# Low parts of the down-projection weights: by a VectorE subtraction, or by a negation and an adding transfer

## The chip, the cores and the metric

The kernel runs on one core of one Trainium2 chip. The metric is the device time of one execution in microseconds, the median of three runs. A profiled execution, taken once more by the hardware profiler, gives the trace that is read here.

## The reference, cut to what matters

The program is a two-layer encoder trunk over 256 frames of width 2048, all in float32. Each layer is a norm, an attention mixer and a residual, then a norm, a gated convolution FFN and a residual. The change lies in the second matrix of the FFN, `w_down`, of 5632 x 2048, in both layers:

```python
def _conv_ffn(xn, w_up, conv_w, conv_b, w_down):
    up = xn @ w_up
    u, g = up[..., :D_FF], up[..., D_FF:]
    g = lax.conv_general_dilated(g, conv_w[:, None, :], window_strides=(1,),
    ...
    return (jax.nn.silu(g) * u) @ w_down
```

## The kernel before

Every large matrix product is made of three products of rounded operands. A float32 operand is split into a high part, its value rounded to the type float32r, and a low part, the float32 value less the high part. TensorE then adds up high x high, high x low and low x high into one PSUM bank. The activations are split once per stage. The weights are streamed from HBM and split as they come, in `stream` (lines 122 to 149).

`stream` loads four k tiles of a weight block at a time, 128 partitions x 4 x 512 float32 (1 MB), into a `raw` buffer (line 130, issued on SP; three buffers rotate). It then goes over the block in steps of two k tiles (KC = 2). In the form that the down product uses, ScalarE copies the two k tiles into `hi` (line 140), a tile of type float32r, and VectorE subtracts `hi` from `raw` into `lo` (line 141). The pool `wsplit` has four buffers for `hi` and four for `lo`, and all weight streams of the kernel share them in order. So the split of a step can begin when the products of the step four before it have read their buffers.

`gemm_tok` (lines 151 to 173) does the products of a step: for each of its two k tiles and each of the two token tiles three matmuls of 512 columns, on lines 158 (high activations, `hi`), 159 (high activations, `lo`) and 160 (low activations, `hi`). These are 12 matmuls per step. The up product runs in `gemm_feat` (lines 183 and 185), with the same `stream`.

In `ffn` (lines 253 to 307) the 5632 hidden features are cut into six groups, five of 1024 and one of 512. `up_group` makes the hidden values of a group: ScalarE copies the side half out of PSUM (line 272), VectorE adds it (line 274), POOL multiplies by the norm factor into `un` (line 276), ScalarE, VectorE and ScalarE do the convolution and the gate (lines 280 to 286), and the result is split into `hT` (lines 287 and 288). `down_group` multiplies a group's `hT` by its rows of `w_down`, for four column blocks of 512, and VectorE adds each block's sum to the residual `h` (line 298). The order in the program is up group 0, then for each next group its up product followed by the down product of the group before, and at the end the last group's down product. A down group of 1024 features has 2 blocks of 1 MB per column block, which are 8 loads and 16 steps; the last one, of 512 features, has 4 loads and 8 steps and follows the fifth one without an up product between. In both layers together these are 88 loads and 176 steps. The last column block of the last group of layer 1 takes its token tiles one after the other (`tok_first`).

The order of instructions on each engine is set when the program is built, by a scheduler that follows the program's order and a simulated timeline. Each engine then works through its own queue in order; SP's queue holds the loads, and POOL's queue holds `un`, the small `pow` operations of the norms and two loads at the start (`pos_i` and `vecs`, lines 368 and 413).

Of the kernel before, what the change touches and what calls it, by code (L numbers as in the profile page):

```python
# [11 lines left out]
F32 = mybir.dt.float32  # L12
F32R = mybir.dt.float32r
I32 = mybir.dt.int32
AF = mybir.ActivationFunctionType
ALU = mybir.AluOpType
# [10 lines left out]
KC = 2  # L27
KD = 4
# [20 lines left out]
def kernel(  # L49
# [7 lines left out]
    vec, act, pool, pe = nc.vector, nc.scalar, nc.gpsimd, nc.tensor  # L57
# [19 lines left out]
    def bank_tile(use, shape, name):  # L77
        pools = turn[use]
        turn[use + "_n"] += 1
        return pools[turn[use + "_n"] % len(pools)].tile(shape, F32, tag=use, name=name)  # L80
# [38 lines left out]

    last = {}  # L120

    def stream(name, src, nk, gain=None, pieces=1, before=None):

        for k0 in range(0, nk, KD):
            raw = wraw.tile([P, KD, CB], F32, tag="raw", name=f"raw_{name}_{k0}")
            for i in range(0, KD, KD // pieces):
                if before:
                    before(k0 + i, KD // pieces)
                part = slice(i, i + KD // pieces)
                last["dma"] = nc.sync.dma_start(raw[:, part, :], src[k0 // KD, :, part, :])  # L130
            for i in range(0, KD, KC):
                nm = f"{name}_{k0 + i}"
                hi = wsplit.tile([P, KC, CB], F32R, tag="whi", name=f"whi_{nm}")
                lo = wsplit.tile([P, KC, CB], F32R, tag="wlo", name=f"wlo_{nm}")
                if gain is None and pieces == KD:
                    for j in range(KC):
                        act.copy(hi[:, j, :], raw[:, i + j, :])
                        vec.tensor_tensor(lo[:, j, :], raw[:, i + j, :], hi[:, j, :].bitcast(F32), ALU.subtract)
                elif gain is None:
                    act.copy(hi, raw[:, i:i + KC, :])  # L140
                    vec.tensor_tensor(lo, raw[:, i:i + KC, :], hi.bitcast(F32), ALU.subtract)  # L141
                else:
                    for j in range(KC):
                        k = k0 + i + j
                        g = gain[:, k:k + 1]
                        act.activation(hi[:, j, :], raw[:, i + j, :], AF.Copy, scale=g)  # L146
                        vec.scalar_tensor_tensor(lo[:, j, :], raw[:, i + j, :], g, hi[:, j, :].bitcast(F32),  # L147
                                                 ALU.mult, ALU.subtract)
                yield k0 + i, hi, lo

    def gemm_tok(name, xt, nk, src, gain=None, pieces=1, before=None, tok_first=False):

        acc = bank_tile("acc", [P, NT, CB], f"acc_{name}")

        def products(k, t, hi, lo):
            xh = xt[:, k, t * P:(t + 1) * P]
            xl = xt[:, k, S + t * P:S + (t + 1) * P]
            pe.matmul(acc[:, t, :], xh, hi, start=k == 0, stop=False)  # L158
            pe.matmul(acc[:, t, :], xh, lo, start=False, stop=False)  # L159
            pe.matmul(acc[:, t, :], xl, hi, start=False, stop=k == nk - 1)  # L160

        steps = ((k0 + j, hi[:, j, :], lo[:, j, :])
                 for k0, hi, lo in stream(name, src, nk, gain, pieces, before) for j in range(KC))
        if tok_first:
            steps = list(steps)
            for t in range(NT):
                for k, hi, lo in steps:
                    products(k, t, hi, lo)
        else:
            for k, hi, lo in steps:  # L170
                for t in range(NT):
                    products(k, t, hi, lo)
        return acc

    def gemm_feat(name, xt, src, pairs, gain=None):

        accs = [bank_tile("acc", [P, 2, CB], f"acc_{name}_{i}") for i in range(len(pairs))]
        for k0, hi, lo in stream(name, src, KT, gain):
            for acc, pair in zip(accs, pairs):
                for m, c in enumerate(pair):  # L180
                    for j in range(KC):
                        k = k0 + j
                        pe.matmul(acc[:, m, :], hi[:, j, c * P:(c + 1) * P], xt[:, k, :],  # L183
                                  start=k == 0, stop=k == KT - 1, skip_group_check=True)
                        pe.matmul(acc[:, m, :S], lo[:, j, c * P:(c + 1) * P], xt[:, k, :S],  # L185
                                  start=False, stop=k == KT - 1, skip_group_check=True)
        return accs
# [55 lines left out]
    def shifted(pool, tag, name, k, shift):  # L243

        t = pool.tile([P, k * 2 * S + PAD], F32R, tag=tag, name=name)
        o = shift // 4
        return t[:, o:o + k * 2 * S].rearrange("p (k s) -> p k s", k=k)
# [5 lines left out]
    def ffn(l, xt, rb, then):  # L253
        up, dn = ((ffn_w_up0, ffn_w_down0), (ffn_w_up1, ffn_w_down1))[l]
        cc = ccols[l]
        groups, f = [], 0
        for n in (4, 4, 4, 4, 4, 2):
            groups.append((f, n))
            f += n
        assert f * 256 == DFF  # L260
        with tc.tile_pool(name=f"ffn{l}", bufs=2) as fp:
            def up_group(gi):
                b0, n = groups[gi]
                hT = shifted(fp, "hT", f"hT{l}_{gi}", 8, HT_SHIFT)
                for b in range(b0, b0 + n):
                    accs = gemm_feat(f"up{l}_{b}", xt, up[b], [(0, 2), (1, 3)])
                    for i, acc in enumerate(accs):
                        ft = 2 * b + i
                        r = 2 * (b - b0) + i
                        nm = f"{l}_{ft}"  # L270
                        side = fp.tile([P, 2, S], F32, tag="side", name=f"side{nm}")
                        act.copy(side, acc[:, :, S:])
                        ug = fp.tile([P, 2, S], F32, tag="ug", name=f"ug{nm}")
                        vec.tensor_tensor(ug, acc[:, :, :S], side, ALU.add)  # L274
                        un = fp.tile([P, 2, S], F32, tag="un", name=f"un{nm}")
                        pool.tensor_tensor(un, ug, rb.unsqueeze(1).broadcast_to([P, 2, S]), ALU.mult)  # L276
                        gn = un[:, 1, :]
                        cv = fp.tile([P, S], F32, tag="cv", name=f"cv{nm}")
                        w = lambda j: cc[:, j * NF + ft:j * NF + ft + 1]
                        act.activation(cv, gn, AF.Identity, scale=w(2), bias=w(3))  # L280
                        vec.scalar_tensor_tensor(cv[:, 1:], gn[:, :S - 1], w(1), cv[:, 1:], ALU.mult, ALU.add)
                        vec.scalar_tensor_tensor(cv[:, 2:], gn[:, :S - 2], w(0), cv[:, 2:], ALU.mult, ALU.add)  # L282
                        sg = fp.tile([P, S], F32, tag="sg", name=f"sg{nm}")
                        act.activation(sg, cv, AF.Silu)  # L284
                        hh = fp.tile([P, S], F32, tag="hh", name=f"hh{nm}")
                        vec.tensor_tensor(hh, sg, un[:, 0, :], ALU.mult)
                        act.copy(hT[:, r, :S], hh)
                        vec.tensor_tensor(hT[:, r, S:], hh, hT[:, r, :S].bitcast(F32), ALU.subtract)
                return hT

            def down_group(gi, hT):
                b0, n = groups[gi]
                for c in range(NB):
                    end = l == 1 and gi == len(groups) - 1 and c == NB - 1
                    acc = gemm_tok(f"dn{l}_{gi}_{c}", hT, 2 * n, dn[c, b0 // 2:(b0 + n) // 2], tok_first=end)
                    for t in range(NT) if end else (slice(0, NT),):
                        hs = h[:, t, c * CB:(c + 1) * CB]
                        vec.tensor_tensor(hs, acc[:, t, :], hs, ALU.add)  # L298
                        if gi == len(groups) - 1:
                            then(c, t)  # L300

            prev = up_group(0)
            for gi in range(1, len(groups)):
                cur = up_group(gi)
                down_group(gi - 1, prev)
                prev = cur
            down_group(len(groups) - 1, prev)
# [57 lines left out]
    with tc.tile_pool(name="mixa", bufs=2) as ap, tc.tile_pool(name="mixa1", bufs=1) as ap1:  # L365
# [12 lines left out]
        for rnd in range(2):  # L378
# [4 lines left out]
            n = ap1.tile([P, NT, 16], F32, name=f"turns_n{rnd}")  # L383
# [171 lines left out]
    with banks("f0", "acc"):  # L555
        _, rb = norm_factor("xf0")
# [85 lines left out]
    with banks("f1", "acc"):  # L642
        _, rb = norm_factor("xf1")
# [67 lines left out]
```

## Time and profile before

| what | value |
|---|---|
| median of 3 runs | 2268.43 us (2267.75 to 2269.35) |
| the profiled execution, its own time | 2269.63 us |
| its span, first to last instruction | 2267.8 us |
| busy: TensorE / VectorE / ScalarE / POOL | 2255.9 / 1443.7 / 1163.3 / 216.9 us |
| mean granted clock of TensorE | 0.999 |
| moved by DMA | 419.85 MB, mean 185 GB/s |

The span is read from the trace, and the execution's own time is 1.8 us longer than it. Busy time counts the instructions of an engine; weight loads of TensorE (PEld) overlap its matmuls (PE). Matmuls overlap each other too: one lasts 0.39 us in the trace, while the next one starts 0.23 us after it. The granted clock is the share of full speed that TensorE was given. "DMA share" is how busy the core's 16 DMA engines were on average.

### The profile page before, as it was taken

To read this page: it belongs to the slowest core of one execution; us is meant where nothing else is said; L and a number is where in the kernel's file an instruction comes from. 1 tells how busy PE (TensorE), PEld (TensorE's weight loads), DVE (VectorE), ACT (ScalarE), POOL (GpSimd) and SP (SyncE) were. 2 spreads that over 40 slices of the span, in tenths; PEclk is the share of its full clock that TensorE was granted. 3 is DMA by queue.
4 is the path that set the end of the run, shared out by engine and by line. 5 is a ranking of instruction groups with operands and counts; after the bars stand their busy time and mean duration, and the time that the engine had idled before them with its cause. 6 is when DMAs were issued, how large, how long until landed. Compare 5 with 4: busy or idle time off the path is not lost.

```text
span 2267.8 us, 29308 instructions
## 1 busy us (share of the span) xinstructions
PE 2255.9 (99%) x11616; PEld 1919.5 (85%) x11616; DVE 1443.7 (64%) x1873; ACT 1163.3 (51%) x1603; POOL 216.9 (10%) x214
## 2 busy tenths in 40 slices
PE   8999999999999999999999999999999999999999
PEld 7888888888888888888888888888888888888887
DVE  8676765666666566666665555556676665757664
ACT  6544455555445454544456756645554444535442
POOL 3111100011000000100001111001110000101000
PEclk9999999999999999999999999999999999999999
DMA  8455445555555555555544454455555555555654
GB/s 285 171 180 173 167 158 183 182 188 191 195 186 186 186 197 193 186 188 189 198 169 166 169 183 169 167 186 173 199 181 193 190 194 190 186 188 183 204 186 149
DMA packets 63210, 419.85 MB, mean 185 GB/s; under 512 B 7072, under 2 KB 9248, under 8 KB 13408
## 3 DMA queue, kind: packets, MB, share of 16 engines
q1 hardware_dynamic: 62816, 417.40, 53.7%
q8 instruction: 91, 1.49, 0.3%
q0 software_dynamic: 112, 0.39, 0.1%
q14 instruction: 47, 0.39, 0.0%
q10 hardware_dynamic: 144, 0.18, 0.0%
HBM read 415.85 MB, written 2.10 MB: 184 GB/s over the span
## 4 chain that ended last, share of the span: by engine, by line
PE 98%; DVE 1%; DMA 1%; ACT 0%; issue 0%; SPq 0%; DVEq 0%
PE acc_up L183 29%; PE acc_up L185 15%; PE acc_dn L158 7%; PE acc_dn L160 7%; PE acc_dn L159 7%; PE acc_k L183 3%; PE acc_q L183 2%; PE acc_k L185 1%; PE acc_bv L158 1%; PE acc_k L159 1%; PE acc_k L158 1%; PE acc_k L160 1%; PE acc_v L158 1%; PE acc_bv L159 1%; PE acc_v L160 1%; PE acc_bv L160 1%
## 5 line engine op out<-in xcount | busy, mean ns | idle before, releaser
L183 PE MATMUL acc_up<-xf,whi_up 128*128 128x512 f32 x2816 | 984.7, 396 | 0.6 <-DVE xf L214 0.6
L185 PE MATMUL acc_up<-xf,wlo_up 128*128 128x256 f32 x2816 | 782.5, 280 | 0.0
L141 DVE TENSOR_TENSOR wlo_up<-raw_up,whi_up 128x1024 fp32r<-128x1024 f32 x352 | 439.2, 1248 | 320.6 <-ACT whi_up L140 320.5
L183 PEld LDWEIGHTS acc_up<-xf,whi_up 128*128 128x128 f32 x2816 | 526.7, 188 | 124.0 <-PE pt_rs_xf L235 0.8
L140 ACT CAST whi_up<-raw_up 128x1024 fp32r<-128x1024 f32 x352 | 369.0, 1048 | 353.2 <-PE acc_up L183 282.6
L185 PEld LDWEIGHTS acc_up<-xf,wlo_up 128*128 128x128 f32 x2816 | 531.4, 189 | 3.5
L141 DVE TENSOR_TENSOR wlo_dn<-raw_dn,whi_dn 128x1024 fp32r<-128x1024 f32 x176 | 217.9, 1238 | 161.7 <-ACT whi_dn L140 161.7
L140 ACT CAST whi_dn<-raw_dn 128x1024 fp32r<-128x1024 f32 x176 | 185.2, 1052 | 242.2 <-PE acc_dn L160 183.1
L160 PE MATMUL acc_dn<-whi_dn,hT 128*128 128x512 f32 x704 | 274.3, 390 | 0.0
L158 PE MATMUL acc_dn<-whi_dn,hT 128*128 128x512 f32 x704 | 274.3, 390 | 0.0
L159 PE MATMUL acc_dn<-wlo_dn,hT 128*128 128x512 f32 x704 | 274.3, 390 | 0.0
L276 POOL TENSOR_TENSOR un<-ug,rsb_xf 128x512 f32<-128x512 f32 x88 | 121.4, 1380 | 1218.6 <-DVE ug L274 1218.6
L160 PEld LDWEIGHTS acc_dn<-whi_dn,hT 128*128 128x128 f32 x704 | 132.2, 188 | 27.5
L158 PEld LDWEIGHTS acc_dn<-whi_dn,hT 128*128 128x128 f32 x704 | 132.2, 188 | 27.4
L159 PEld LDWEIGHTS acc_dn<-wlo_dn,hT 128*128 128x128 f32 x704 | 132.2, 188 | 27.1
L284 ACT ACTIVATE sg<-cv 128x256 f32<-128x256 f32 x88 | 36.6, 416 | 110.2 <-DVE cv L282 110.2
L183 PE MATMUL acc_k<-xb,whi_k 128*128 128x512 f32 x256 | 90.9, 397 | 0.0
L183 PE MATMUL acc_q<-xb,whi_q 128*128 128x512 f32 x256 | 89.5, 396 | 0.0
L282 DVE SCALAR_TENSOR_TENSOR cv<-un,cols,cv 128x254 f32<-128x254 f32 x88 | 82.8, 941 | 3.1
L298 DVE TENSOR_TENSOR h<-acc_dn,h 128x1024 f32<-128x1024 f32 (+1 forms) x49 | 58.9, 1203 | 23.0 <-PE acc_dn L160 22.2
L185 PE MATMUL acc_k<-xb,wlo_k 128*128 128x256 f32 x256 | 72.2, 283 | 0.0
L147 DVE SCALAR_TENSOR_TENSOR wlo_q<-raw_q,cols,whi_q 128x512 fp32r<-128x512 f32 x64 | 46.9, 777 | 38.2 <-ACT whi_q L146 38.2
(290 smaller groups left out, 3188.9 us busy)
## 6 DMA issues: line engine op xcount, KB each, us to landing
raw_up<-in_ffn_w_up_dram SPq DMA_DIRECT2D x176, 1024.0 KB, 4.8
raw_dn<-in_ffn_w_down_dram SPq DMA_DIRECT2D x88, 1024.0 KB, 4.8
raw_k<-in_a_w_qkv_dram SPq DMA_DIRECT2D x16, 1024.0 KB, 4.8
raw_v<-in_a_w_qkv_dram SPq DMA_DIRECT2D x16, 1024.0 KB, 4.8
raw_ao<-in_a_w_o_dram SPq DMA_DIRECT2D x16, 1024.0 KB, 4.8
raw_k<-in_b_w_kv_dram SPq DMA_DIRECT2D x16, 1024.0 KB, 4.8
raw_q<-in_b_w_q_dram SPq DMA_DIRECT2D x16, 1024.0 KB, 5.0
raw_bv<-in_b_w_kv_dram SPq DMA_DIRECT2D x16, 1024.0 KB, 4.8
```

The source lines that it names most:

```text
L140: act.copy(hi, raw[:, i:i + KC, :])
L141: vec.tensor_tensor(lo, raw[:, i:i + KC, :], hi.bitcast(F32), ALU.subtract)
L147: vec.scalar_tensor_tensor(lo[:, j, :], raw[:, i + j, :], g, hi[:, j, :].bitcast(F32), ALU.mult, ALU.subtract)
L158: pe.matmul(acc[:, t, :], xh, hi, start=k == 0, stop=False)
L159: pe.matmul(acc[:, t, :], xh, lo, start=False, stop=False)
L160: pe.matmul(acc[:, t, :], xl, hi, start=False, stop=k == nk - 1)
L183: pe.matmul(acc[:, m, :], hi[:, j, c * P:(c + 1) * P], xt[:, k, :], start=k == 0, stop=k == KT - 1, skip_group_check=True)
L185: pe.matmul(acc[:, m, :S], lo[:, j, c * P:(c + 1) * P], xt[:, k, :S], start=False, stop=k == KT - 1, skip_group_check=True)
L276: pool.tensor_tensor(un, ug, rb.unsqueeze(1).broadcast_to([P, 2, S]), ALU.mult)
L282: vec.scalar_tensor_tensor(cv[:, 2:], gn[:, :S - 2], w(0), cv[:, 2:], ALU.mult, ALU.add)
L284: act.activation(sg, cv, AF.Silu)
L298: vec.tensor_tensor(hs, acc[:, t, :], hs, ALU.add)
```

## The change

`gemm_tok` and `stream` get an argument `add`, which the down product sets. With it ScalarE writes the negated high part into `lo`, and a DMA issued by POOL reads the same two k tiles of the weights a second time from HBM and adds them to what stands in `lo`. The values are the same: the weights less the high part.

```diff
-    def stream(name, src, nk, gain=None, pieces=1, before=None):
+    def stream(name, src, nk, gain=None, pieces=1, before=None, add=False):
...
+                elif gain is None and add:
+                    act.copy(hi, raw[:, i:i + KC, :])
+                    act.activation(lo, hi.bitcast(F32), AF.Copy, scale=-1.0)
+                    pool.dma_start(out=lo, in_=src[k0 // KD, :, i:i + KC, :], accum_op=ALU.add)
                 elif gain is None:
                     act.copy(hi, raw[:, i:i + KC, :])
                     vec.tensor_tensor(lo, raw[:, i:i + KC, :], hi.bitcast(F32), ALU.subtract)
...
-    def gemm_tok(name, xt, nk, src, gain=None, pieces=1, before=None, tok_first=False):
+    def gemm_tok(name, xt, nk, src, gain=None, pieces=1, before=None, tok_first=False, add=False):
...
-                 for k0, hi, lo in stream(name, src, nk, gain, pieces, before) for j in range(KC))
+                 for k0, hi, lo in stream(name, src, nk, gain, pieces, before, add) for j in range(KC))
...
-                    acc = gemm_tok(f"dn{l}_{gi}_{c}", hT, 2 * n, dn[c, b0 // 2:(b0 + n) // 2], tok_first=end)
+                    acc = gemm_tok(f"dn{l}_{gi}_{c}", hT, 2 * n, dn[c, b0 // 2:(b0 + n) // 2], tok_first=end, add=True)
```

## Rows read from the trace of the kernel before

**Rows 1.** The page: span, busy time and share of each engine; the chain by engine.

```profile
span 2267.8 us, 29308 instructions
PE 2255.9 (99%) x11616; PEld 1919.5 (85%) x11616; DVE 1443.7 (64%) x1873; ACT 1163.3 (51%) x1603; POOL 216.9 (10%) x214
...
PE 98%; DVE 1%; DMA 1%; ACT 0%; issue 0%; SPq 0%; DVEq 0%
```

**Rows 2.** The page's costliest groups: count, busy us, mean ns, idle before and releaser.

```profile
L141 DVE TENSOR_TENSOR wlo_dn<-raw_dn,whi_dn 128x1024 fp32r<-128x1024 f32 x176 | 217.9, 1238 | 161.7 <-ACT whi_dn L140 161.7
L140 ACT CAST whi_dn<-raw_dn 128x1024 fp32r<-128x1024 f32 x176 | 185.2, 1052 | 242.2 <-PE acc_dn L160 183.1
```

**Rows 3.** Windows (up, down, up): length, busy us per engine, clock, DMA share, GB/s.

```profile
core 0: us, PE busy (x) PEld busy (x) DVE busy (x) ACT busy (x) POOL busy (x), PEclk, DMA share, GB/s
564.00:587.00 23.00, 23.00 (x129) 19.89 (x128) 15.71 (x20) 11.64 (x16) 2.76 (x2) 1.00 0.54 183
587.00:630.00 43.00, 43.00 (x194) 35.68 (x194) 28.07 (x29) 18.68 (x21) 1.46 (x1) 1.00 0.57 196
630.00:653.00 23.00, 23.00 (x132) 19.96 (x131) 10.97 (x11) 10.01 (x11) 1.29 (x1) 1.00 0.53 183
```

**Rows 4.** Timeline of TensorE in a down stretch: start us, duration us; twelve matmuls apart.

```profile
611.99 0.39 PE L158 MATMUL acc_dn<-whi_dn,hT 128*128 128x512 f32 x1
612.22 0.39 PE L159 MATMUL acc_dn<-wlo_dn,hT 128*128 128x512 f32 x1
...
614.71 0.39 PE L158 MATMUL acc_dn<-whi_dn,hT 128*128 128x512 f32 x1
```

**Rows 5.** Timeline of ScalarE: first copy for the stretch, a small cast, copies within.

```profile
575.74 1.05 ACT L140 CAST whi_dn<-raw_dn 128x1024 fp32r<-128x1024 f32 x1 [1.82 <-PE acc_up L183]
...
590.98 0.40 ACT L287 CAST hT<-hh 128x256 fp32r<-128x256 f32 x1
...
606.07 1.05 ACT L140 CAST whi_dn<-raw_dn 128x1024 fp32r<-128x1024 f32 x1 [1.66 <-PE acc_dn L160]
608.79 1.05 ACT L140 CAST whi_dn<-raw_dn 128x1024 fp32r<-128x1024 f32 x1 [1.67 <-PE acc_dn L160]
```

**Rows 6.** Waits of SP's queue: us in total, times, longest us.

```profile
SPq L130 <- DVE wlo_dn L141: 376.2, 75, 5.4
```

**Rows 7.** Timeline of POOL: its two DMA issues at the start.

```profile
1.69 0.75 POOL L368 DMA_DIRECT2D pos_i<-in_positions_dram  x1
3.23 0.57 POOL L413 DMA_DIRECT2D vecs<-in_vectors_dram  x1
```

**Rows 8.** Waits of the engines: us in total, times, longest us.

```profile
POOL un L276 <- DVE ug L274: 1218.6, 88, 61.6
```

**Rows 9.** DMA issues: count, KB each, median us from issue to landing.

```profile
raw_dn<-in_ffn_w_down_dram SPq DMA_DIRECT2D x88, 1024.0 KB, 4.8
...
out_dram<-h SPq DMA_DIRECT2D x3, 512.0 KB, 2.8
out_dram<-h SPq DMA_DIRECT2D x2, 256.0 KB, 2.2
vecs<-in_vectors_dram POOLq DMA_DIRECT2D x1, 384.0 KB, 6.4
...
pos_i<-in_positions_dram POOLq DMA_DIRECT2D x1, 1.0 KB, 3.7
```

**Rows 10.** DMA page of the down stretch 587 to 630 us, 40 slices of 1.075 us.

```profile
GB/s 107 236 412 236 0 0 122 404 404 46 69 198 412 297 0 84 198 427 267 0 61 191 427 305 0 69 168 442 297 15 23 191 389 373 0 15 168 381 404 8
```

**Rows 11.** Timeline of TensorE: the first matmul of the down stretch.

```profile
584.09 0.39 PE L158 MATMUL acc_dn<-whi_dn,hT 128*128 128x512 f32 x1
```

**Rows 12.** Windows early in the kernel, columns as in rows 3.

```profile
10.00:20.00 10.00, 9.11 (x38) 6.79 (x37) 9.87 (x33) 9.52 (x19) 0.70 (x1) 1.00 1.02 353
34.00:36.00 2.00, 0.39 (x2) 0.35 (x3) 2.00 (x2) 1.99 (x5) 1.92 (x2) 1.00 0.85 356
36.00:38.00 2.00, 2.00 (x8) 1.62 (x7) 2.00 (x2) 1.82 (x2) 1.92 (x2) 0.74 0.00 0
38.00:40.00 2.00, 2.00 (x6) 1.54 (x5) 2.00 (x3) 0.41 (x1) 0.38 (x1) 0.50 0.60 127
```

**Rows 13.** Timeline of TensorE after its wait near 34 us.

```profile
35.61 0.50 PE L159 MATMUL acc_k<-wlo_k,xa 128*128 128x512 f32 x1 [1.99 <-DVE wlo_k L141]
...
38.07 0.63 PE L158 MATMUL acc_k<-whi_k,xa 128*128 128x512 f32 x1
38.50 0.63 PE L159 MATMUL acc_k<-wlo_k,xa 128*128 128x512 f32 x1
```

## The prediction

> **What bounds the kernel now.** I read the page's busy shares and chain first: TensorE is busy 99% of a 2267.8 us span, and 98% of the chain that ended last lies on it; VectorE is at 64%, ScalarE at 51% [rows 1]. So taking work from VectorE shortens nothing by itself; the change can only matter by making TensorE wait, or not. The groups by cost then give the pieces that it touches: 176 subtractions on VectorE of 1.238 us (217.9 us in all) and 176 copies on ScalarE of 1.052 us [rows 2]. The windows show one down stretch between two up stretches: TensorE is full in all three, at full clock, and the DMA engines are a little over half busy at 183 to 196 GB/s [rows 3]. In a down stretch the matmuls start 12 per step (two k tiles, two token tiles, three products): the same product comes again after 2.72 us [rows 4]. ScalarE's copies come at this same 2.72 us, each released by the last product that read the buffer four steps back [rows 5]. That is the kernel's slack: four pairs of hi and lo buffers, so a low part may be late by nearly 4 x 2.72 = 10.88 us after its buffer came free, less the matmuls' own 2.72 us.
>
> **The change, part by part.** *Removed:* 176 VectorE subtractions, 217.9 us [rows 2]. They lie beside TensorE; worth 0. SP's next weight load, which waited for the subtraction [rows 6], can start after ScalarE's copy, some 1.2 us sooner; the loads are up to three buffers ahead, so this too is worth 0.
>
> *Added on ScalarE:* 176 negations. Their nearest row is the copy of the same 128x1024 tile, 1.052 us; they can hardly cost below the 0.40 us of a cast a quarter of its size [rows 5] or above twice the copy. I take 1.05 us, 185 us in all. In the full down stretch ScalarE is busy 18.68 of 43 us [rows 3]; 16 negations bring 16.8 us, so 35.5 of 43. TensorE covers it; without that cover a step would still need only 2.1 us of ScalarE against 2.72 us.
>
> *Added on POOL:* 176 issues of 0.57 to 0.75 us, by the two that POOL makes at the start [rows 7]; some 130 us, beside TensorE. In POOL's queue stand the multiplications `un`, two per up block; they now stand behind an issue that waits for ScalarE's negation. ScalarE's `cv` waits for `un`, but `un` waited 1218.6 us for VectorE in sum [rows 8], and the tile made from it is read only one down stretch later; I cost this at 0, with 1 us per stretch (10 us) as the upper end.
>
> *Added on the path:* every low part now takes copy, negation, issue and a transfer, where it took copy and subtraction. The loop from a buffer's release to its next release is: hand-over about 0.3 us, 1.05 + 1.05 us, landing time L, matmuls 2.72 us, so about 5.1 + L. It is hidden while it is at most 10.88 us, so while **L is at most 5.8 us**. No row has an adding transfer. From below: 1 KB issued by POOL lands after 3.7 us, and a 512 KB store after 2.8 us, against 2.2 us for half of that [rows 9]; 3.7 us and 524 KB at 404 GB/s (1.3 us) make 5.0. From above: 384 KB issued by POOL, beside other loads, took 6.4 us [rows 9], and the additions run beside a stream of 1 MB loads of 4.8 us each.
>
> *Added on the DMA engines*, and this is the term that I take to decide. A pair of steps needs one 1 MB load in 2 x 2.72 = 5.44 us; two slices in a row that a load fills move 404 GB/s [rows 10], so a load takes 1.049 MB / 404 GB/s = 2.60 us of the engines: 48% (the window says 0.57 busy). The change adds per step a transfer that must fetch 0.524 MB of weights and also fetch the 0.524 MB in the tile, and write the sum. Lower bound: the second fetch is free, 1.30 us per step; upper: two fetches and the write each take their turn, 3.9 us; below nothing is excluded, since bytes are added. I take two fetches, 2.60 us per step, because two input streams have to come in through the engines while the write leaves as a plain load's does. Then a pair costs 3 x 2.60 = 7.80 us of DMA against 5.44 us of TensorE: **the down stretches become DMA bound**.
>
> The Trainium skill says the same price from another place: "Collectives: The Full Stack", section on why ReduceScatter is half of AllGather, has an adding transfer at half the rate because both sources are read on one side of the engine. No run here shows it.
>
> *The sum.* Each layer has four stretches of 16 steps and one of 24 (the last two groups follow each other). The first copy of a stretch starts at 575.74 and the first matmul at 584.09 [rows 5, 11]; with copy and negation, 2.1 us, the transfers start 6.3 us ahead of the matmuls. Between then and the last sum the engines have 8 loads and 16 additions, 24 units of 2.60 = 62.4 us (36 units, 93.6 us, in the long one). After that come 2.2 us of fixed landing time (4.8 less 2.6) and the last step's 2.72 us. So a stretch lasts 62.4 - 6.3 + 2.2 + 2.7 = 61.0 us instead of 43.5, and the long one 92.2 instead of 65.3: +17.5 and +26.9 us. Per layer 4 x 17.5 + 26.9 = 96.9, for two layers +194 us. The profiled execution took 2269.6 us by its own time (1.8 us more than its span, 1.2 above the median), so 2463 for it, and **2462 us** for the median. With 442 GB/s, the best slice [rows 10], the unit is 2.37 us and the sum +133 us (2402 us); with 353 GB/s, the longest saturated stretch [rows 12], it is 2.97 us and +292 us (2560 us). So this case's own range is 2402 to 2560, and I keep 404 because it is the same stage and the same queue.
>
> **The rivals.** *Hidden (not slower).* If the second fetch is free and L stays within 5.8 us, every addition lands before its step: 2268 us. For it: 5.0 us by the lower row, and two units per pair, 5.2 us, just fit in 5.44. Against it: 3.7 us for 1 KB leaves only 2.1 us for 0.5 MB beside another stream. The point of decision is L = 5.8 us.
>
> The Trainium skill's "DMA: Bandwidth & Descriptors", section on the anatomy of one DMA, fits a transfer of this path as 2.0 us and the bytes at 436 GB/s, an estimate of 3.2 us here, which would be this rival. The row of 1 KB at 3.7 us already lies above that.
>
> *Latency only.* The second fetch is free but the loop isn't: with L = 5.0 plus one load in the way (2.6) = 7.6 us a loop takes 12.7 us per four steps, 1.8 too many; 136 steps follow the four made ahead in each of the ten stretches, 34 loops, +62 us: 2330 us (L = 6.4 gives 2289).
>
> *Slower still.* The addition takes three turns: per pair 4 units, 10.4 us, and by the same sum +38.3 and +58.1 us per stretch, +423 us: 2691 us. The same price has another mechanism: where TensorE waited 1.99 us for a low part near 34 us, the granted clock went to 0.50 some 1.3 us after that wait, its lower level of 1.2 GHz, and matmuls started every 0.43 us instead of 0.23 [rows 12, 13]. Were that to hold for all 176 steps, they would take 12 x 0.43 = 5.1 us instead of 2.72: +420 us, and no more, since slower matmuls let the transfers catch up.
>
> *Faster.* Only if a wait on VectorE were on the chain; VectorE holds 1% of it [rows 1]. *The addition is not made as one transfer* (split or dropped): a plain copy would be the latency case in time.
>
> **How the numbers follow.** DMA bound as summed 0.45; latency only 0.17; slower still 0.23; hidden 0.12; faster 0.03. A change of 0.2%, 4.5 us, is about what a measurement of this kernel can tell. Slower is 0.45 + 0.17 + 0.23 = 0.85, same 0.12, faster 0.03. The range takes in the hidden, the latency and the DMA bound case and reaches part of the way to 2691: 2267 to 2650 leaves out about 0.2.
>
> **What would show it.** Right: TensorE waiting for `wlo_dn` at the product of line 159 some 180 to 200 us in sum, only in down stretches; a down window near 61 us with a DMA share near 1; some 92 MB more on the software queue (more, if both fetches are counted); `wlo_dn` transfers landing in about 10 us from issue. A DMA share well under 1 with landings of 6 to 8 us is the latency case; granted clock near 0.5 in down windows is the clock's part. Wrong altogether: no waits of TensorE at all, or a DMA share near 1 with a sum beyond 2650 us.

## The result and the profile after

The changed kernel takes 2471.11 us (2465.21 to 2476.12) against 2268.64 us: 8.9% slower, a ratio of 1.0893 with an interval of 1.0875 to 1.0910. The forecast was 2462 us.

The page of the changed kernel: busy times, the chain by engine and by line, the queues, and the groups that answer to [rows 2] and [rows 9].

```profile
PE 2320.8 (94%) x11616; PEld 1932.2 (78%) x11616; DVE 1232.2 (50%) x1697; ACT 1342.1 (54%) x1779; POOL 365.9 (15%) x390
...
q1 hardware_dynamic: 62816, 417.40, 48.2%
q0 software_dynamic: 25456, 92.68, 19.3%
...
PE 73%; DMA 20%; issue 4%; DVE 2%; ACT 1%; POOL 0%; SPq 0%; DVEq 0%; POOLq 0%; ACTq 0%
...
L163 PE MATMUL acc_dn<-wlo_dn,hT 128*128 128x512 f32 x704 | 300.4, 427 | 132.1 <-DMA wlo_dn<-in_ffn_w_down_dram 131.3
L163 PEld LDWEIGHTS acc_dn<-wlo_dn,hT 128*128 128x128 f32 x704 | 138.8, 197 | 204.2 <-DMA wlo_dn<-in_ffn_w_down_dram 177.4
L142 POOL DMA_DIRECT2D wlo_dn<-in_ffn_w_down_dram x176 | 153.0, 869 | 558.5 <-ACT wlo_dn L141 459.7
L141 ACT ACTIVATE wlo_dn<-whi_dn 128x1024 fp32r<-128x1024 f32 x176 | 186.3, 1058 | 4.6
...
raw_dn<-in_ffn_w_down_dram SPq DMA_DIRECT2D x88, 1024.0 KB, 8.8
wlo_dn<-in_ffn_w_down_dram POOLq DMA_DIRECT2D x176, 512.0 KB, 9.6
```

VectorE is freed of some 212 us (1443.7 to 1232.2), and the kernel got 197 us longer in span. The chain, 98% TensorE before [rows 1], now has 20% DMA. Among the matmuls, TensorE's one new idle group is the one that uses the low part (line 163 now, 159 before), and its releaser is the adding transfer. A wait shows twice, once at the matmul (131.3 us) and once at its weight load (177.4 us); they overlap and are not to be added. A 1 MB load of down weights lands after 8.8 us, before it was 4.8 [rows 9].

The windows of the first down stretch (61 us, the length of the forecast) and of its pieces in the changed kernel, columns as in [rows 3]:

```profile
584.00:645.00 61.00, 49.71 (x194) 38.14 (x193) 11.75 (x16) 32.84 (x37) 14.58 (x16) 0.92 1.01 266
584.00:590.00 6.00, 3.24 (x15) 2.40 (x13) 3.86 (x7) 5.70 (x9) 4.26 (x5) 0.94 1.04 275
590.00:600.00 10.00, 9.98 (x31) 7.97 (x32) 1.50 (x4) 4.44 (x7) 1.59 (x2) 0.69 1.05 265
600.00:610.00 10.00, 7.35 (x31) 5.38 (x30) 1.22 (x1) 6.13 (x7) 2.63 (x3) 1.00 1.04 292
640.00:650.00 10.00, 10.00 (x51) 8.40 (x51) 4.02 (x5) 3.48 (x4) 0.00 (x0) 1.00 0.58 156
```

The DMA share is 1.04 to 1.05 through the stretch and falls to 0.58 as it ends. A share over 1 means that packets overlap on an engine. During 97% of the time that TensorE waits for `wlo_dn` in the whole run, 16 or more packets are open, so the engines have work all along.

The order of TensorE's queue changed too. Before, the 192 matmuls of a short down stretch stood together; now the scheduler has put 21 matmuls of the next up product between them, 2 in front of the first product that needs the last addition but one, and 19 in front of the first that needs the last. It is so in all eight short stretches. Here are the first of the 19 and the product behind them:

```profile
643.68 0.28 PE L189 MATMUL acc_up<-xf,wlo_up 128*128 128x256 f32 x1
...
646.98 0.39 PE L163 MATMUL acc_dn<-wlo_dn,hT 128*128 128x512 f32 x1
```

The last product of the first stretch thus ends at 649.6 us and not by 645, with 3.8 us of up matmuls inside the stretch.

Between 584 and 640 us the engines show only 265 to 292 GB/s, below the 404 of [rows 10]. The DMA page of the stretch from 600 to 636 us explains that: queue, packets, MB, share of 16 engines.

```profile
GB/s 428 350 200 196 214 214 269 337 387 314 314 237 191 214 237 337 364 319 319 287 200 200 214 309 360 332 319 323 214 196 209 278 328 360 328 305 255 200 209 246
q0 software_dynamic: 1385, 5.08, 71.0%
q1 hardware_dynamic: 677, 4.89, 33.5%
```

The two queues carry nearly the same bytes, but the additions take 71% of the engines and the loads 33.5%. Per addition of 0.524 MB that is 0.710 x 36 us x 0.524 / 5.08 = 2.64 us, per load of 1.049 MB 0.335 x 36 x 1.049 / 4.89 = 2.59 us. The profile counts the bytes of an addition once, while the engines are busy for twice as long per byte. A pair of steps thus needs 2.59 + 2 x 2.64 = 7.87 us of the engines, against 5.44 us of TensorE. A pair in fact took 7.4 us (5.08 MB of additions in 36 us); the difference is the overlap, 7.87 / 1.05 = 7.5.

The single packets give the same price: an addition is 128 packets of 4096 bytes, and the median one is open for 328 ns, 128 x 0.328 / 16 = 2.62 us.

### The profile page after: what moved, and what is told of

The parts are those of the page before. It is cut to its first block, busy times and chain, and to the rows that moved or that the text cites. A ratio compares the mean times of both kernels' runs of the same rounds, so it can differ in the third digit from the quotient of the medians.

```text
span 2464.6 us, 29784 instructions
## 1 busy us (share of the span) xinstructions
PE 2320.8 (94%) x11616; PEld 1932.2 (78%) x11616; DVE 1232.2 (50%) x1697; ACT 1342.1 (54%) x1779; POOL 365.9 (15%) x390
## 4 chain that ended last, share of the span: by engine, by line
PE 73%; DMA 20%; issue 4%; DVE 2%; ACT 1%; POOL 0%; SPq 0%; DVEq 0%; POOLq 0%; ACTq 0%
PE acc_up L187 23%; DMA wlo_dn<-in_ffn_w_down_dram 19%; PE acc_up L189 11%; PE acc_dn L163 4%; PE acc_dn L164 3%; PE acc_dn L162 3%; PE acc_k L187 2%; PE acc_q L187 2%; PE acc_k L189 1%; PE acc_bv L162 1%; PE acc_k L163 1%; PE acc_k L164 1%; PE acc_k L162 1%; PE acc_v L164 1%; PE acc_v L162 1%
## 5 line engine op out<-in xcount | busy, mean ns | idle before, releaser
L163 PE MATMUL acc_dn<-wlo_dn,hT 128*128 128x512 f32 x704 | 300.4, 427 | 132.1 <-DMA wlo_dn<-in_ffn_w_down_dram 131.3
L163 PEld LDWEIGHTS acc_dn<-wlo_dn,hT 128*128 128x128 f32 x704 | 138.8, 197 | 204.2 <-DMA wlo_dn<-in_ffn_w_down_dram 177.4
L164 PE MATMUL acc_dn<-whi_dn,hT 128*128 128x512 f32 x704 | 287.2, 408 | 0.0
L162 PE MATMUL acc_dn<-whi_dn,hT 128*128 128x512 f32 x704 | 280.6, 406 | 0.0
L142 POOL DMA_DIRECT2D wlo_dn<-in_ffn_w_down_dram x176 | 153.0, 869 | 558.5 <-ACT wlo_dn L141 459.7
L141 ACT ACTIVATE wlo_dn<-whi_dn 128x1024 fp32r<-128x1024 f32 x176 | 186.3, 1058 | 4.6
L162 PEld LDWEIGHTS acc_dn<-whi_dn,hT 128*128 128x128 f32 x704 | 139.7, 198 | 32.5
L164 PEld LDWEIGHTS acc_dn<-whi_dn,hT 128*128 128x128 f32 x704 | 140.2, 199 | 26.6
L278 DVE TENSOR_TENSOR ug<-acc_up,side 128x512 f32<-128x512 f32 x88 | 60.1, 683 | 98.6 <-ACT side L276 98.6
L286 DVE SCALAR_TENSOR_TENSOR cv<-un,cols,cv 128x254 f32<-128x254 f32 x88 | 73.6, 837 | 3.1
```

The lines of the kernel that those rows point to most:

```text
L141: act.activation(lo, hi.bitcast(F32), AF.Copy, scale=-1.0)
L142: pool.dma_start(out=lo, in_=src[k0 // KD, :, i:i + KC, :], accum_op=ALU.add)
```

## The experiments

All times are medians beside runs of the kernel before on the same chip (2268.3 to 2269.0 us).

**Half of the additions.** Does the loss follow the load on the engines or the wait of each addition?

```diff
-                elif gain is None and add:
+                elif gain is None and add and i == 0:
```

> Only every second step of the down product takes its low part from the adding transfer; the others keep the VectorE subtraction. Theory (the transfers' own time on the 16 DMA engines is the bound, some 2.64 us per addition and 2.60 us per 1 MB load): a pair of steps now needs 2.60 + 2.64 = 5.24 us of the engines, just under the 5.44 us of its matmuls, so the loss nearly vanishes: 2268 to 2290 us. Rival (the loop through four buffers with a fixed landing time of 9.6 us is the bound): an adding step still comes back only after 5.1 + 9.6 = 14.7 us instead of 10.88, in 34 loops: +130 us, about 2400 us.

Measured: 2320.66 us, ratio 1.0222 (1.0205 to 1.0239). Both numbers are wrong. The DMA page of this run from 600 to 624 us, and the landing times of all its additions:

```profile
DMA  9999520007879997999967999989979899999999
q1 hardware_dynamic: 564, 4.15, 45.6%
q0 software_dynamic: 486, 1.73, 43.3%
...
DMA to landing us min/median/max: 5.3/6.0/9.2
```

By the page an addition takes 0.433 x 24 x 0.524 / 1.73 = 3.15 us here, not 2.64, and a load 2.77 us: 5.9 us per pair, above 5.44. But this isn't a lack of engines. The DMA share is 0.89, in three slices nothing moves, and 16 or more packets are open in only 71% of the time that TensorE waits, against 97% in the changed kernel. The median packet of an addition is open for 328 ns as there; the mean rises by a tail, 10% of the packets that are open for over 0.5 us, against 1% there. Landing fell from 9.6 to 6.0 us (median, the last line), so the fixed 9.6 us of the rival falls too. Still, 48 of the 88 additions land after more than the 5.8 us that the four buffers hide. That this is what costs the 52 us is likely, but no run separates it.

**A quarter of the additions**, with these units:

```diff
-                elif gain is None and add:
+                elif gain is None and add and k0 == 0 and i == 0:
```

> Only the first step of each weight block group in a column block takes its low part from the adding transfer, 48 of the 176 steps; the rest keep the VectorE subtraction. Theory (DMA bound; the run with every second step measured 3.15 us per addition beside 2.8 us per load, 5.9 us against 5.44): four steps now need 2 x 2.8 + 3.15 = 8.8 us of 10.88, the engines have room, so 2268 to 2280 us, the upper end for additions that land over 5.8 us after their issue. Rival (each addition costs a share of its own, 52 us for 88 of them): 48 of them +28 us, 2297 us.

Measured: 2275.12 us, ratio 1.0034 (1.0020 to 1.0048). With 48, 88 and 176 additions the loss is 7, 52 and 202 us: 0.14, 0.59 and 1.15 us for each. That isn't a price per addition, and the theory's range holds. Landing is 5.5 us in the median, and 3 of the 48 additions land after more than 5.8 us. The additions' queue on the page of this run, which the last section uses:

```profile
q0 software_dynamic: 7024, 25.56, 6.8%
```

**The transfer without the addition.**

```diff
-                    pool.dma_start(out=lo, in_=src[k0 // KD, :, i:i + KC, :], accum_op=ALU.add)
+                    pool.dma_start(out=lo, in_=src[k0 // KD, :, i:i + KC, :])
```

> The same transfer without the addition: it copies the weights over the negated high parts (the subtraction is left out, so the low part is the weight itself). Theory (the second fetch costs the engines as much as the first): 1.3 us of all engines per transfer instead of 2.7, a pair needs 5.2 of 5.44 us, so 2268 to 2330 us, the upper end if latency shows. Rival (a transfer issued by POOL in rows of 4 KB costs 2.7 us whatever it does): 2471 us as with the addition.

Measured: 2350.27 us, ratio 1.0352 (1.0330 to 1.0374). Its queues from 600 to 624 us:

```profile
q0 software_dynamic: 1108, 4.06, 50.1%
q1 hardware_dynamic: 540, 3.90, 43.8%
```

The same bytes cost 0.501 x 24 x 0.524 / 4.06 = 1.55 us per transfer instead of 2.64, and 121 of the 202 us are gone: the addition itself costs the engines 1.1 us per transfer. By the median packet it is 174 ns instead of 328. The rival falls. The time lies 20 us above the range. By the page a load takes 2.83 us here and a pair 5.9 us, but the share is 0.94, and by median packets (309 ns for 8192 bytes of a load) a pair needs only 2.47 + 2 x 1.39 = 5.25 us, under 5.44. The median landing is 6.5 us, and 125 of the 176 transfers land after more than 5.8. So this looks like the latency case, for which the prediction named a plain copy and 2330 us; that too is argued and not separated. POOL's issue is shorter, 0.53 us against 0.87 (medians).

In its section on why ReduceScatter is half of AllGather, the Trainium skill's "Collectives: The Full Stack" has a transfer that adds at half the rate of one that copies. The traces here come near it: 2.64 / 1.55 = 1.7 by the pages, 328 / 174 = 1.9 by the median packets. That the second fetch is what takes the time, and not the adding, no run here separates.

**The weights from SBUF.**

```diff
-                    pool.dma_start(out=lo, in_=src[k0 // KD, :, i:i + KC, :], accum_op=ALU.add)
+                    pool.dma_start(out=lo, in_=raw[:, i:i + KC, :], accum_op=ALU.add)
```

> The adding transfer takes the weights from the raw buffer in SBUF, where the load has put them, not a second time from HBM. Theory (two fetches through the DMA engines are the price, wherever they come from): the engines stay full in the down stretches and the time stays at 2471, within 20 us. Rival (reading HBM twice is the price): below 2350 us. A raw buffer is now held until the addition has landed, which can only lengthen it.

Measured: 2456.08 us, ratio 1.0820 (1.0802 to 1.0838). The page's queue of the additions and the bytes from HBM:

```profile
q0 software_dynamic: 25456, 92.68, 19.8%
...
HBM read 415.85 MB, written 2.10 MB: 170 GB/s over the span
```

HBM is read no more than before the change (415.85 MB there too), and an addition still takes 0.198 x 2454.4 / 176 = 2.76 us of the engines; the same sum gives 2.70 for the changed kernel. The time is 15 us under that of the changed kernel, within the 20 that I gave. What is short is the engines, not HBM.

**The wait without the bytes.**

```diff
-                    pool.dma_start(out=lo, in_=src[k0 // KD, :, i:i + KC, :], accum_op=ALU.add)
+                    pool.dma_start(out=lo[:, :, :64], in_=src[k0 // KD, :, i:i + KC, :64], accum_op=ALU.add)
```

> The adding transfer moves only the first 64 of each 512 columns (the rest of the low part stays the negated high part), while copy, negation, issue and the wait for the landing all stay. Theory (DMA bound): landing 4 to 5 us, under the 5.8 us that the four buffers hide, so 2268 to 2275 us. Rival (the longer chain through ScalarE, POOL and the wait costs, whatever the bytes): more than 2350 us.

Measured: 2286.39 us, ratio 1.0080 (1.0065 to 1.0095). Landing is 3.7 us (median) and 2.9 to 6.9. So 185 of the 202 us go with the bytes. 17 us stay, more than expected. TensorE's waits in the down product are 11 there, 11.8 us in all. Nine of them, 10.1 us, one in every stretch but the ninth, end with the landing of the stretch's fifth addition, which took 6.4 to 6.6 us each time. That is above the 5.8 us that the four buffers hide. The chain of waits at the first of them, start and length in us:

```profile
586.27 0.52 POOL un L280
586.79 0.71 issue
587.50 1.20 POOL wlo_dn L142
588.70 0.82 issue
589.53 6.41 DMA wlo_dn<-in_ffn_w_down_dram
596.08 0.47 PE acc_dn L163
```

Two runs tried to name their cause. The first moves `un` off POOL, the second the negation off ScalarE, both with the 64-column addition:

```diff
-                        pool.tensor_tensor(un, ug, rb.unsqueeze(1).broadcast_to([P, 2, S]), ALU.mult)
+                        vec.tensor_tensor(un, ug, rb.unsqueeze(1).broadcast_to([P, 2, S]), ALU.mult)
```

> The run with the 64-column addition (the rest of the low part stays the negated high part) left +17 us. Here the multiplication un goes from POOL to VectorE as well. Theory (the additions stand behind un in POOL's queue where a down stretch begins, and un waits for ScalarE and VectorE): the rest goes, 2268 to 2274 us. Rival (ScalarE, which now copies and negates, is late by itself): it stays at 2283 to 2288 us.

Measured: 2288.47 us, ratio 1.0088 (1.0073 to 1.0103).

```diff
-                    act.activation(lo, hi.bitcast(F32), AF.Copy, scale=-1.0)
+                    vec.tensor_scalar(lo, hi.bitcast(F32), -1.0, None, ALU.mult)
```

> The run with the 64-column addition, the negation of the high part made by VectorE instead of ScalarE (un stays on POOL). By the POOL queue theory 2283 to 2288 us, as with ScalarE's negation; by the rival (ScalarE's double work is late) 2268 to 2274 us.

Measured: 2289.96 us, ratio 1.0097 (1.0082 to 1.0112). The 17 us stayed both times, so neither POOL's `un` nor ScalarE's double work is their cause by itself. The first edit leaves the fifth addition late (6.4 to 6.7 us); with the second most waits move to the seventh. What is left is the late landing of about one addition per stretch, 6.4 us and more against a median of 3.7, and why it is late stays open.

**More work for TensorE**, in the changed kernel and in the one before (`zero` is a tile of zeros):

```diff
...
+            if name.startswith("dn"):
+                pe.matmul(acc[:, t, :], zero, hi, start=False, stop=False)
             pe.matmul(acc[:, t, :], xl, hi, start=False, stop=k == nk - 1)
```

> The changed kernel with one more matmul per k tile and token tile in the down product (a zero tile times the high part, into the same sum): 704 matmuls more at 0.227 us, 160 us of TensorE. Theory (DMA bound): a step's matmuls grow from 2.72 to 3.63 us, still under the 3.9 us that the DMA engines need per step, so TensorE uses up its waiting time and the time stays within 30 us of 2471; the granted clock rises. Rival (the waits are a loop of latencies, with the matmuls one link of it): 44 loops longer by 0.9 us, about 2511 us. Rival (TensorE is still the bound outside a few waits): 2631 us.

> The same 704 matmuls in the kernel before, as the control: TensorE is full there, so all of them show: 2269 + 160 = 2429 us by either theory.

Measured: 2503.46 us for the changed kernel, 32 us more, and 2438.88 us for the one before, 170.6 us more. The windows of the first down stretch with the added matmuls:

```profile
584.00:645.00 61.00, 57.98 (x250) 45.88 (x249) 11.39 (x16) 33.11 (x37) 14.69 (x16) 1.00 1.02 266
```

Where TensorE is the bound, 704 matmuls cost 170.6 us; where the engines are, four fifths of that goes into the waiting time. TensorE is busy 58 of 61 us and not 49.7, and the granted clock is 1.00 and not 0.92. 32 us is just over the 30 that I gave, and near enough to the rival's 2511 that this run doesn't separate DMA engines from a loop of latencies. The next one does.

**Five pairs of buffers**, with two raw buffers for three to make room:

```diff
-    wraw = ctx.enter_context(tc.tile_pool(name="wraw", bufs=3))
-    wsplit = ctx.enter_context(tc.tile_pool(name="wsplit", bufs=4))
+    wraw = ctx.enter_context(tc.tile_pool(name="wraw", bufs=2))
+    wsplit = ctx.enter_context(tc.tile_pool(name="wsplit", bufs=5))
```

> The changed kernel with five pairs of split buffers instead of four, paid for by two raw buffers instead of three. Theory (DMA bound): the engines need 7.8 to 8 us per pair of steps as before; one more addition is made ahead in each of ten stretches, at most 26 us less: 2445 to 2475 us. Rival (the loop of latencies with a landing time of 9.6 us): (5.1 + 9.6) / 5 = 2.94 us per step instead of 3.7, so about 2310 us.

> The same buffers in the kernel before, as the control: 2268 to 2275 us by either theory, if two raw buffers are enough for TensorE there; what it loses is to be taken off the other run.

Measured: 2448.83 us for the changed kernel, and 2268.99 us, unchanged (ratio 1.0002, 0.9992 to 1.0011), for the one before. The issues' landing times by tile in this run:

```profile
DMA to landing us min/median/max: 8.4/12.5/15.5
```

The window of its first down stretch:

```profile
584.00:645.00 61.00, 50.10 (x202) 38.46 (x203) 13.19 (x16) 32.10 (x36) 12.95 (x14) 0.94 1.01 272
```

A loop of latencies would have gone to 2310. Instead the landing time rose from 9.6 to 12.5 us at the same DMA share of 1.01: one more addition in flight mostly waits longer for the engines. Landing here is a result of the load, not a cause. The 22 us that are gained lie within the 26 us forecast for one more addition made ahead in each stretch.

**`un` on VectorE in the changed kernel.** The edit is that of the first of the two small runs above.

> The changed kernel with un on VectorE instead of POOL. Theory (DMA bound in the down stretches): the additions at the start of a stretch are issued a few us sooner, at most some 1.5 us in each of ten stretches: 2455 to 2475 us. Rival (the 2.8 us wait at the start of the stretch, and the low clock after it, is what sets the stretch): below 2430 us.

Measured: 2469.20 us, ratio 1.0885 (1.0868 to 1.0901). Nothing changed, and neither did the wait at the start of the stretch (first line the changed kernel, second this run):

```profile
590.02 0.79 PE L163 MATMUL acc_dn<-wlo_dn,hT 128*128 128x512 f32 x1 [2.78 <-DMA wlo_dn<-in_ffn_w_down_dram]
590.40 0.80 PE L163 MATMUL acc_dn<-wlo_dn,hT 128*128 128x512 f32 x1 [2.86 <-DMA wlo_dn<-in_ffn_w_down_dram]
```

So `un` on POOL isn't what TensorE waits for there. The rival of this run is not tested by it, because the wait and the low clock behind it stayed (0.89 in the first stretch, 0.92 before this edit). The run with the added matmuls says more on it: its first stretch has a granted clock of 1.00 and 64 matmuls more, and from its first matmul to that of the second down stretch it takes 153.2 us, against 151.6 in the changed kernel. In the kernel before, the same matmuls lengthen that way from 133.2 to 148.8 us. So TensorE's pace isn't what sets it here.

None of these kernels beats the kernel before.

## Why the prediction was right

*What bounds it.* TensorE at 99% meant that VectorE's 218 us could bring nothing, and they brought nothing: the run with the small addition is rid of them too, and ends 17 us above the kernel before.

*The term that decides* was the engines' time per transfer: I took 2.60 us per load and 2.60 per addition, with 1.30 and 3.9 as the ends. Measured under full load are 2.59 and 2.64. That the price is on the engines is shown by the runs with SBUF as source (no less) and without the addition (1.55 us). That the engines are the bound is shown by the five buffers and by the added matmuls, which the waits took up.

*The sum.* The transfers' part came out: from the issue of a stretch's first addition to the landing of its last one it is 64.9 to 65.8 us in the short stretches, against 62.4 + 2.2 = 64.6. The lead over the first matmul is 5.7 to 5.9 us instead of 6.3. The end was not foreseen: from the last landing to the end of the last product it takes 5.0 to 6.4 us instead of 2.7, since up matmuls now stand before it, and these are then missing from the up stretch. From the ends of the stretches in the two traces, the eight short stretches grew by 16.9 to 21.8 us, 18.8 on average, against 17.5 forecast; the two long ones by 23.1 and 23.5, against 26.9. Together 8 x 18.8 + 2 x 23.3 = 197 us, against 194. In the medians it is 202 us. The errors have both signs and nearly cancel, so it is luck that the sum came this close. What `un` behind POOL's issues costs I had put at 0, with 10 us over all as the upper end, and moving it changed nothing. The longer chain as a whole had no other term; the run with the small addition makes it up to 17 us.

*POOL's order.* I had `un` behind an issue that waits for the negation. That is half of it: the first `un`, at 584.91, follows such an issue (583.86), but what it waits for is VectorE's `ug`. The other half I left out: the next addition is issued behind both `un`, at 587.81. Moving `un` changed nothing, so this was without price. POOL's issue takes 0.869 us, above the 0.57 to 0.75 that I took from plain transfers [rows 7]; also without price.

The timeline of POOL at the start of the first down stretch shows it:

```profile
583.86 0.87 POOL L142 DMA_DIRECT2D wlo_dn<-in_ffn_w_down_dram  x1 [1.88 <-ACT wlo_dn L141]
584.91 1.28 POOL L280 TENSOR_TENSOR un<-ug,rsb_xf 128x512 f32<-128x512 f32 x1 [0.18 <-DVE ug L278]
586.59 1.28 POOL L280 TENSOR_TENSOR un<-ug,rsb_xf 128x512 f32<-128x512 f32 x1 [0.40 <-DVE ug L278]
587.81 0.89 POOL L142 DMA_DIRECT2D wlo_dn<-in_ffn_w_down_dram  x1
```

*The negation*, 1.058 us against 1.05, is hidden as forecast: the run with the small addition holds all 176 of them and is only 17 us over the kernel before, which moving them to VectorE didn't change.

*The rivals.* Hidden: no, landing is 9.6 us and not under 5.8. Latency only, which was to end near 2330: no, by the run with five buffers; the plain copy, which the prediction put there, ended at 2350. Slower still by three turns: no, 2.64 us is two turns. Slower still by the clock: the mechanism is there (0.69 granted from 590 to 600, after a wait of 2.78 us), but it holds for little. The mean clock of 0.985 is worth 0.015 x 2464.6 = 37 us of the whole execution, an estimate, and not 420; and from 590 to 600 us, where the clock is low, the DMA share stays at 1.05, so the slower matmuls use up waiting time. *Faster*: nothing on VectorE was on the chain.

*What would show it.* TensorE waited for `wlo_dn` at the named product and in down stretches alone, 131 us by its matmuls and 177 us by their weight loads (the two overlap) against 180 to 200; the DMA share was 1.01 over the 61 us; 92 MB came on the software queue; landing was 9.6 us against about 10.

## What to carry to other kernels

Before work is moved from a compute engine to a transfer, add up the DMA engines' time per step of the stage that it goes into, with an adding transfer counted at about twice a copy (328 ns against 174 per packet here), and compare it with the bound engine's time there: here 7.9 us had to fit into 5.44 us, although the DMA share there was only 0.57 before [rows 3]. If the landing time grows with a buffer more and the share stays at 1, the transfers are the bound, and more buffers help little (22 of 202 us here). If there is room on the engines, the landing time still has to fit into what the buffers hide. And an engine with idle time beside a full one, like VectorE at 64% beside TensorE at 99%, needs no relief.

## What the runs showed that was not expected

By the pages the DMA engines' time per transfer seems to depend on the load: an addition of 0.524 MB took 2.64 us with 176 of them, 3.15 us with 88, and 0.068 x 2273.3 / 48 = 3.22 us with 48. The packets show that the price is the same, a median of 328 ns in all three, and that a tail grows: 1%, 10% and 12% of the packets are open for more than 0.5 us. A share of busy time counts this tail as work. My expectation for half of the additions, 2268 to 2290 us, thus did not fail by its prices, but because it took room on the engines for enough. The loss goes with the additions that land after more than 5.8 us: 3 of 48 in the run with a quarter (7 us), 13 of 176 in the one with 64 columns (17 us), 48 of 88 with half (52 us), 125 of 176 with the plain copy (81 us), 167 of 176 in the changed kernel (202 us), where the late landing is itself the work of the full engines.

The GB/s of a stretch also misleads where additions run: 266 GB/s at a share of 1.01 looks like slow engines, but an addition's bytes are counted once, while its packets are open for nearly twice as long as those of a copy. And a small addition of 64 columns is dearer to issue on POOL than a large one, 1.20 us against 0.87; why was not tried.
